# Another fixed order for the experts' ranks of load in a routed mixture of experts

## The chip, the core and the metric

The kernel runs on one core of one Trainium2 chip. It is measured in microseconds of device time for one execution; of several runs the median counts. Slower or faster always means this time.

## What is computed

One call computes two transformer blocks over 256 tokens of width 1024 in fp32. The first block mixes a short convolution, a gated delta rule and a stick-breaking attention, and has a dense feed-forward part; the second has two attentions and then a mixture of 32 experts. Only the mixture bears on this change:

```python
logits = hf @ w_router + b_router              # 256 tokens, 32 experts
top_val, top_idx = lax.top_k(logits, 4)        # each token goes to 4 experts
gates = softmax(top_val)
for each expert e, for the tokens x that chose it:
    hh = x @ w1[e] + b1[e]                     # 1024 -> 2048
    y  = swiglu_clamped(hh) @ w2[e] + b2[e]    # 1024 -> 1024
out[token] = sum of gate * y over its 4 experts
```

The weights of one expert (w1 of 8 MB and w2 of 4 MB) are read once, whatever the number of its tokens. The sum over the experts can be taken in any order.

## The kernel before

The dense parts come first and take a little over a third of the time. After the router the kernel counts the tokens of each expert and ranks the experts by that count; ranks 0 and 1 are fixed to experts 0 and 1, the others go from the largest load to the smallest. Each rank has a fixed number of slots, its capacity, from the table `CAPS`: ranks 0 and 1 have 64, ranks 2 and 3 have 128, ranks 4 to 7 have 96, ranks 8 to 17 have 64, ranks 18 to 31 have 32. Which expert stands at a rank is known only at run time; the program for each rank is written out in full. A loop at the end (line 1940) treats experts with more tokens than slots.

`ORDER` lists the ranks in the sequence in which the loop at line 1826 takes them; `pos` below is the place in that list. For each rank the loop emits:

- `selects` for the next rank (VectorE makes the one-hot matrices that pick its tokens and its gates),
- `first_rounds` of this rank: the product with w1, in blocks. `cut` cuts a capacity into blocks of 64 and 32 slots: 64 is one block, 96 is a block of 64 and one of 32, 128 is two blocks of 64. A block of 64 has two rounds, the first of slabs 0 and 1, the second of slabs 2 and 3; a block of 32 has one round, of all four. The matmuls stand at line 1725. Before the last round of a rank the next rank's tokens are gathered (line 1683),
- `turn` for the next rank: its tokens are transposed and normalised (lines 1694 to 1703),
- `combine` of the rank before: its output goes into the sum over experts (line 1791),
- `second` of this rank: the product with w2, for blocks of 64 at line 1768, of 32 at line 1763.

The weights come in slabs of 2 MB, six for each rank: four of w1, two of w2. Ten slab buffers stand in SBUF. All slabs are loaded by one queue of DMA issues on SyncE (SP), in the order in which they will be used, by `load_m` (the DMA stands at line 246). A slab buffer is given back by `free_m`, which `first_rounds` and `second` call behind the matmuls that read the slab last, so only in the rank's last block; it then emits the load of the slab that comes ten places later into the same buffer:

```python
def free_m(keys):
    for k in keys:
        del m_slab[k]
        m_freed.add(m_num.pop(k))
    while state["freed"] in m_freed:
        load_m(state["next"], m_pool[state["freed"]])
        state["next"] += 1
        state["freed"] += 1
```

The load waits on SP until TensorE has done those matmuls, and the loads behind it in the queue wait too. Numbered over the whole mixture, the slabs are 0 to 191, and slab n + 10 takes the place of slab n.

Of the kernel before, what the change touches and what calls it, by code (L numbers as in the profile page):

```python
# [48 lines left out]

FIRST = 2  # L50
CAPS = [64] * 2 + [128] * 2 + [96] * 4 + [64] * 10 + [32] * 14
ORDER = [0, 1, 8, 18, 9, 2, 26, 10, 3, 27, 11, 4, 28, 12, 5, 19, 13, 6, 29, 14, 7, 20, 15, 30, 21, 16, 22, 17, 23, 24, 25,
         31]


N_DENSE = 67
# [110 lines left out]
def kernel(ctx: ExitStack, tc: tile.TileContext, x_in, cols_in, rows_in, const_in, cona_in, conb_in, rpb_in,  # L167
# [62 lines left out]
    def load_m(m, pool=None):  # L230

        pos, i = divmod(m, 6)
        if pos >= len(ORDER):
            return
        rank = ORDER[pos]
        i = ((0, 2, 1, 3) if CAPS[rank] == 32 else (0, 1, 2, 3))[i] if i < 4 else i
# [1556 lines left out]
    def by_rank(rank):  # L1793
        if rank < FIRST:
            return lambda c: place[:, c, rank:rank + 1], lambda c: gate[:, c, rank:rank + 1]
        return lambda c: rp[:, 0, c, rank:rank + 1], lambda c: rp[:, 1, c, rank:rank + 1]

    def selects(pos):
        rank = ORDER[pos]
        pos_, gate_ = by_rank(rank)  # L1800
        return [select(w, first, tb, pos_, gate_ if pos else None) for first, tb in cut(CAPS[rank])]
# [23 lines left out]
    pend = []  # L1825
    for pos, rank in enumerate(ORDER):
        m0_ = 6 * pos
# [7 lines left out]
        n = 0  # L1835
        last = pos + 1 == len(ORDER)

# [263 lines left out]
```

## Time and profile before

| | us |
|---|---|
| median of 3 runs | 1496.65 (1492.77 to 1497.12) |
| the profiled execution | 1493.93 |
| its span, first to last instruction | 1492.1 |
| TensorE (PE) busy in the span | 1370.7 (92%) |
| VectorE (DVE) busy | 546.6 (37%) |
| ScalarE (ACT) busy | 455.9 (31%) |
| 192 slabs of experts' weights, 2048 KB each | 384 MB |
| first matmul with experts' weights | starts at 547.7 |

Times in the views count from the start of the span. TensorE's busy share is taken from modelled ends of its instructions, so the share is read with care. The mixture lies between 548 us and the end; the first ten slabs are on their way before it starts.

### The profile page before, as it was taken

The numbers are of one execution on the slowest core, as the hardware profiler recorded it, in microseconds if no ns is written. First come the engines' busy times: TensorE is split into PE (matmuls) and PEld (weight loads), VectorE is DVE, ScalarE is ACT, GpSimd is POOL, SyncE is SP. The second block draws the span as 40 slices with busy tenths as digits, with TensorE's granted clock in tenths as the row PEclk, the third lists the DMA queues.
The fourth block names the chain that finished last, engine by engine and source line by source line (L and its number), as shares of the span: only waits on it lengthen the run. The fifth ranks groups of instructions, "written<-read, shape, count | busy, mean of one in ns | idle before, by whom it ended". The sixth has DMA issues, their size and how long they took to land.

```text
span 1492.1 us, 21744 instructions
## 1 busy us (share of the span) xinstructions
PE 1370.7 (92%) x8859; PEld 736.1 (49%) x8863; DVE 546.6 (37%) x1258; ACT 455.9 (31%) x979; POOL 55.6 (4%) x31
## 2 busy tenths in 40 slices
PE   7999999999899999999999999999999987887674
PEld 6899789998678753333333333333333322222121
DVE  4755678776757841222122122112112111111112
ACT  5564465555556641111111111112111111101111
POOL 2322010000000000000000000000000000000000
PEclk9999999999999999999999999999999998989887
DMA  8322586656774599999899899999999999999994
GB/s 314 113 92 107 186 330 248 258 200 228 260 277 174 179 390 402 424 427 421 345 429 417 346 427 417 426 426 427 428 427 428 427 427 427 428 427 427 428 427 186
DMA packets 43433, 506.66 MB, mean 340 GB/s; under 512 B 5024, under 2 KB 5280, under 8 KB 6880
## 3 DMA queue, kind: packets, MB, share of 16 engines
q1 hardware_dynamic: 42464, 503.49, 82.5%
q10 hardware_dynamic: 864, 1.72, 0.4%
q8 instruction: 72, 1.18, 0.3%
q14 instruction: 33, 0.27, 0.0%
HBM read 504.14 MB, written 1.05 MB: 339 GB/s over the span
## 4 chain that ended last, share of the span: by engine, by line
PE 74%; DMA 17%; ACT 4%; DVE 3%; issue 1%; POOL 0%; SPq 0%; ACTq 0%; DVEq 0%; POOLq 0%
PE mm L1725 23%; DMA w<-in_we 16%; PE mm L447 15%; PE mm L1768 9%; PE acc L1791 4%; PE mm L1683 3%; PE mm L1763 3%; PE acc L481 3%; PE acc L482 3%; PE acc L483 3%; DMA w<-in_ws 1%; PE mm L824 1%; ACT aT L1746 1%; PE mm L1694 1%; PE mm L1730 1%
## 5 line engine op out<-in xcount | busy, mean ns | idle before, releaser
L1725 PE MATMUL mm<-w,xT 128*64 128x512 f32 (+1 forms) x2432 | 449.4, 642 | 56.3 <-DMA w<-in_we 56.0
L1725 PEld LDWEIGHTS mm<-w,xT 128*64 128x64 f32 (+1 forms) x2432 | 134.1, 131 | 354.2 <-issue 279.6
L1734 DVE TENSOR_SCALAR h<-mm 128x256 f32<-128x256 f32 x58 | 24.6, 425 | 714.8 <-PE mm L1730 714.8
L447 PE MATMUL mm<-hT,u 128*128 128x256 f32 x2064 | 263.5, 287 | 1.4 <-DVE hT L436 0.6
L447 PEld LDWEIGHTS mm<-hT,u 128*128 128x128 f32 x2064 | 254.1, 193 | 12.8 <-issue 8.4
L1735 ACT ACTIVATE a<-h 128x256 f32<-128x256 f32 x58 | 24.2, 417 | 506.0 <-DVE h L1734 506.0
L408 DVE TENSOR_TENSOR u<-w,u 128x1024 fp32r<-128x1024 f32 x115 | 145.5, 1270 | 67.3 <-ACT u L403 67.3
L403 ACT ACTIVATE u<-w 128x1024 fp32r<-128x1024 f32 x134 | 139.9, 1056 | 34.0 <-PE acc L483 23.9
L1768 PE MATMUL mm<-w,aT 128*64 128x512 f32 x640 | 143.2, 600 | 5.3 <-ACT aT L1746 5.3
L1768 PEld LDWEIGHTS mm<-w,aT 128*64 128x64 f32 x640 | 44.5, 138 | 91.2 <-issue 81.0
L1773 ACT ACTIVATE y<-mm 128x512 f32<-128x512 f32 x38 | 22.7, 597 | 208.6 <-PE mm L1768 139.8
L1763 PE MATMUL mm<-w,aT 128*32 128x512 f32 x576 | 65.5, 595 | 9.9 <-ACT aT L1746 9.9
L1683 PE MATMUL mm<-x,S 128*32 128x256 f32 (+1 forms) x448 | 57.4, 463 | 2.5 <-DVE S L1670 2.5
L408 POOL TENSOR_TENSOR u<-w,u 128x1024 fp32r<-128x1024 f32 x19 | 46.8, 2465 | 330.5 <-PE mm L306 201.4
L1063 DVE SCALAR_TENSOR_TENSOR fcv<-mm,cols,fcv 128x255 f32<-128x255 f32 x88 | 42.3, 481 | 22.9 <-ACT fcv L1060 21.4
L1701 ACT ACTIVATE xT<-mm,mod,gs 128x64 f32<-128x64 f32 (+1 forms) x152 | 46.6, 386 | 2.1 <-PE mm L1694 1.5
L1703 DVE TENSOR_SCALAR xT<-mm,gs,mod 128x64 f32<-128x64 f32 (+1 forms) x152 | 38.7, 321 | 3.0 <-PE mm L1694 3.0
L1763 PEld LDWEIGHTS mm<-w,aT 128*32 128x32 f32 x576 | 16.8, 109 | 46.5 <-issue 31.1
L1683 PEld LDWEIGHTS mm<-x,S 128*32 128x32 f32 (+1 forms) x448 | 18.7, 119 | 39.6 <-issue 33.1
L1926 POOL TENSOR_TENSOR fs<-fs,x 128x512 f32<-128x512 f32 x1 | 1.3, 1259 | 946.9 <-ACT fr L314 946.9
L1060 ACT ACTIVATE fcv<-mm,cols 128x256 f32<-128x256 f32 x44 | 20.7, 471 | 50.8 <-PE mm L447 50.8
L481 PE MATMUL acc<-u,gh 128*128 128x512 f32 x88 | 34.9, 397 | 0.0
(546 smaller groups left out, 1374.5 us busy)
## 6 DMA issues: line engine op xcount, KB each, us to landing
w<-in_we SPq DMA_DIRECT2D x192, 2048.0 KB, 23.3
w<-in_ws SPq DMA_DIRECT2D x90, 1024.0 KB, 5.3
nb<-in_rpb SPq DMA_DIRECT2D x4, 512.0 KB, 7.7
x<-in_x SPq DMA_DIRECT2D x2, 512.0 KB, 6.1
w<-in_ws SPq DMA_DIRECT2D x2, 512.0 KB, 7.5
bt<-in_b SPq DMA_DIRECT2D x3, 256.0 KB, 8.5
out<-fs SPq DMA_DIRECT2D x3, 256.0 KB, 2.1
grow<-in_wf ACTq DMA_DIRECT2D x1, 512.0 KB, 4.9
```

What stands on the lines that cost most here:

```text
L403: nc.scalar.activation(hi, raw, AF.Copy)
L408: eng.tensor_tensor(lo, raw, hi, op=OP.subtract)
L447: nc.tensor.matmul(b[:, 0:T], w[:, k, :], h[:, k, :], start=(n == 0), stop=(n == 3 * KC - 1))
L481: nc.tensor.matmul(o, th[:, kc, t], wh[:, w], start=first, stop=False)
L482: nc.tensor.matmul(o, th[:, kc, t], wl[:, w], start=False, stop=False)
L483: nc.tensor.matmul(o, tl[:, kc, t], wh[:, w], start=False, stop=last)
L1683: nc.tensor.matmul(b[p * tb:(p + 1) * tb, 0:n], S[:, c, p * tb:(p + 1) * tb], x[:, c, p * n:(p + 1) * n], start=(c == 0), stop=(c == 1))
L1701: nc.scalar.activation(dst, src, AF.Identity, scale=gs[:, kc:kc + 1], bias=mod[:, 24 + kc:25 + kc])
L1725: nc.tensor.matmul(b[p * tb:(p + 1) * tb, :], xT[:, k, q * tb:(q + 1) * tb], w1(p * nr + rd, kc // 4)[:, kc % 4, :], start=(kc == 0), stop ...
L1763: nc.tensor.matmul(b[p * tb:(p + 1) * tb, :], aT[:, 0, j, p0 * tb:(p0 + 1) * tb], w2(bi)[:, j, h * 512:(h + 1) * 512], start=(bi == 0), st ...
L1768: nc.tensor.matmul(b[p * tb:(p + 1) * tb, :], aT[:, rd, j, p0 * tb:(p0 + 1) * tb], w2(bi)[:, j, p * 512:(p + 1) * 512], start=(bi == 0 and ...
L1791: nc.tensor.matmul(acc[c][h], lhsT, rhs, start=False, stop=False, skip_group_check=True)
```

## The change

The list `ORDER` is replaced by another permutation of the same 32 ranks. Nothing else is changed: the capacities, the slabs, the buffers, the instructions of each rank and the code that stands at fixed places of the loop (after `pos` 0, 2, 3 and 6) stay. Ranks 0 and 1 remain first and rank 31 remains last.

```diff
 FIRST = 2
 CAPS = [64] * 2 + [128] * 2 + [96] * 4 + [64] * 10 + [32] * 14
-ORDER = [0, 1, 8, 18, 9, 2, 26, 10, 3, 27, 11, 4, 28, 12, 5, 19, 13, 6, 29, 14, 7, 20, 15, 30, 21, 16, 22, 17, 23, 24, 25,
-         31]
+ORDER = [0, 1, 18, 19, 8, 9, 10, 20, 2, 21, 22, 23, 4, 24, 11, 12, 5, 25, 6, 26, 13, 27, 7, 14, 15, 28, 3, 29, 30,
+         16, 17, 31]
```

Written as capacities, by `pos` from 0 to 31:

```
before: 64 64 64 32 64 128 32 64 128 32 64 96 32 64 96 32 64 96 32 64 96 32 64 32 32 64 32 64 32 32 32 32
after:  64 64 32 32 64 64 64 32 128 32 32 32 96 32 64 64 96 32 96 32 64 32 96 64 64 32 128 32 32 64 64 32
```

## Rows read from the trace of the kernel before

**Rows 1.** The page: rate of DMA in 40 slices; the slabs' issues, KB, us to landing.

```profile
GB/s 314 113 92 107 186 330 248 258 200 228 260 277 174 179 390 402 424 427 421 345 429 417 346 427 417 426 426 427 428 427 428 427 427 427 428 427 427 428 427 186
w<-in_we SPq DMA_DIRECT2D x192, 2048.0 KB, 23.3
```

**Rows 2.** Chain that ended last, from 1200 us: start, us, what.

```profile
1207.69 7.09 PE mm L1768 x32
...
1215.75 39.07 DMA w<-in_we
```

**Rows 3.** Windows: busy us of PE, PEld, DVE, ACT, POOL; PE clock, DMA, GB/s.

```profile
695.00:745.00 50.00, 49.36 (x284) 17.11 (x282) 9.23 (x28) 7.85 (x22) 0.00 (x0) 1.00 0.88 365
745.00:795.00 50.00, 48.17 (x248) 16.80 (x246) 10.33 (x35) 7.69 (x20) 0.00 (x0) 1.00 1.01 428
795.00:840.00 45.00, 44.36 (x258) 15.24 (x256) 7.90 (x23) 6.74 (x19) 0.00 (x0) 1.00 0.86 351
...
885.00:910.00 25.00, 24.74 (x166) 8.44 (x162) 6.46 (x20) 3.64 (x11) 0.00 (x0) 1.00 0.99 409
910.00:1215.00 305.00, 295.49 (x1844) 100.57 (x1846) 62.23 (x202) 51.84 (x143) 0.00 (x0) 1.00 1.01 427
1215.00:1462.00 247.00, 185.63 (x1081) 57.05 (x1073) 31.83 (x102) 28.71 (x79) 0.00 (x0) 0.87 1.01 427
```

**Rows 4.** Waits of the SP queue, 704 to 731 us: total, times, longest us.

```profile
SPq L246 <- PE mm L1768: 14.7, 1, 14.7
```

**Rows 5.** Issue and landing (us later) of slabs 17, 35, 43 and 44.

```profile
L246 SPq DMA_DIRECT2D w<-in_we x1: 333/333/333, 587.8 to 587.8; - x1
DMA to landing us min/median/max: 10.1/10.1/10.1
...
L246 SPq DMA_DIRECT2D w<-in_we x1: 333/333/333, 661.9 to 661.9; - x1
DMA to landing us min/median/max: 24.7/24.7/24.7
...
L246 SPq DMA_DIRECT2D w<-in_we x1: 331/331/331, 714.7 to 714.7; - x1
DMA to landing us min/median/max: 11.6/11.6/11.6
...
L246 SPq DMA_DIRECT2D w<-in_we x1: 333/333/333, 730.0 to 730.0; - x1
DMA to landing us min/median/max: 9.0/9.0/9.0
```

**Rows 6.** PE in order of time, first round of experts: start, us.

```profile
580.67 7.09 PE L1725 MATMUL mm<-w,xT 128*64 128x512 f32 x32
...
607.26 7.04 PE L1725 MATMUL mm<-w,xT 128*64 128x512 f32 x32
...
637.82 8.02 PE L1725 MATMUL mm<-w,xT 128*32 128x512 f32 x64
...
654.80 7.09 PE L1725 MATMUL mm<-w,xT 128*64 128x512 f32 x32
...
685.21 7.04 PE L1725 MATMUL mm<-w,xT 128*64 128x512 f32 x32
...
735.02 7.07 PE L1725 MATMUL mm<-w,xT 128*32 128x512 f32 x64
...
751.23 7.09 PE L1725 MATMUL mm<-w,xT 128*64 128x512 f32 x32
...
877.45 7.04 PE L1725 MATMUL mm<-w,xT 128*64 128x512 f32 x32
...
892.60 7.05 PE L1725 MATMUL mm<-w,xT 128*32 128x512 f32 x64
...
916.72 7.07 PE L1725 MATMUL mm<-w,xT 128*32 128x512 f32 x64
```

**Rows 7.** PE in order of time from 1240 us: a capacity-64 expert behind a wait.

```profile
1270.25 8.78 PE L1725 MATMUL mm<-w,xT 128*64 128x512 f32 x32 [2.93 <-DMA w<-in_we]
```

## The prediction

> **What bounds the kernel now.** I read the page first, then the chain that ended last, the windows of the mixture, the SP queue's waits, single slab issues, and TensorE in order of time. The page shows a DMA rate of about 427 GB/s through most of the mixture, with dips to 345 and 346 [rows 1]. The chain shows two regimes. Up to 1215 us it runs over TensorE; from 1215.75 us on it runs over the slab loads [rows 2]. So the end is set by when the last slab lands, and the last slab lands when the queue has moved 384 MB: any time in which the queue had nothing to move is in the total. In the windows the full rate is 428 GB/s [rows 3]. Below that lie, before the DMA-bound tail:
>
> - 695 to 745 us: 365 GB/s, so 50 x (1 - 365/428) = 7.4 us lost
> - 795 to 840 us: 351 GB/s, so 45 x (1 - 351/428) = 8.1 us lost
> - 885 to 910 us: 409 GB/s, so 25 x (1 - 409/428) = 1.1 us lost
>
> Together 16.6 us. From 910 to 1215 us the rate is 427, at most 0.7 us lost; the tail is at 427 too. The page's slice from 559.5 to 596.9 us has 402 GB/s [rows 1], another 37.3 x (1 - 402/428) = 2.3 us, at `pos` 0 and 1, which both orders share.
>
> The reader is to see in the SP queue why: the queue's longest wait in 704 to 731 us is 14.7 us, for the second product's matmul [rows 4]. That is `pos` 5, a rank of 128 slots. It gives its slabs back only in its second block, and its w2 slabs only at its end. Ten buffers are full by then.
>
> **A rule for a stall, from the rows.** A slab takes 2048 x 1024 bytes / 428 GB/s = 4.9 us, an expert six of them, 29.4 us. A slab issued into an empty queue landed 9.0 us after its issue [rows 5]. Let x be the time from a rank's first matmul to the landing of its sixth slab (negative: landed before). The 128 at `pos` 5 starts at 685.2 [rows 6]; its sixth slab, number 35, landed at 661.9 + 24.7 = 686.6 [rows 5], so x = 1.4. Its first w2 buffer came free at 730.0, 44.8 us after the start, and the load into it, slab 44, landed at 44.8 + 9.0 = 53.8. At an unbroken rate it was due nine slabs behind the sixth: x + 44.1 = 45.5. So 8.3 us are lost; the rows show slab 43 at 714.7 + 11.6 = 726.3 and slab 44 at 739.0 [rows 5], 12.7 us apart where 4.9 are due: 7.8 lost. The rule fits. From it:
>
> - 128 slots: no stall if x is at least 53.8 - 44.1 = 9.7.
> - 96 slots: its first slabs come free half way through its second block, at 892.6 + 3.5 - 877.45 = 18.7 us [rows 6], and land at 27.7; due at x + 24.5. No stall from x = 3.2 up.
> - 64 and 32 slots: a slab is free 3.6 us after the start, lands at 12.6, due at x + 24.5. No stall from x = -11.9 up.
>
> **What a rank does to x.** x grows by 29.4 less the rank's period, first matmul to first matmul. Periods in which TensorE waited for no load [rows 6]: 64 slots 607.26 - 580.67 = 26.6; 32 slots 751.23 - 735.02 = 16.2, and 17.0 at `pos` 3; 128 slots 735.02 - 685.21 = 49.8; 96 slots 916.72 - 877.45 = 39.3. A rank in front of a two-block rank takes 3.8 us more, for the larger gather and turn (64 before 128: 685.21 - 654.80 = 30.4); I take the same behind 32. A first matmul can't run before its first slab, so x is at most 5 x 4.9 = 24.5; past that TensorE waits and the loads run at full rate.
>
> **The change, part by part.** The list alone changes. Each rank issues the same instructions and the same six loads, in the one SP queue, so nothing is removed or added: bytes, matmuls and the tail behind rank 31 are the same, and those cost nothing more. What moves is where x stands at each rank. The loop's fixed work behind `pos` 2 now follows a rank of 32; before, the next rank's period was preceded by one of 30.6 (637.82 - 607.26) where a 64 takes 26.6 [rows 6], so I charge 17 + 4 = 21 us at most, 18 as the value nearest to the rows of a 32, to `pos` 2.
>
> The new ledger. `pos` 2 starts as before: slab 17 landed at 587.8 + 10.1 = 597.9 [rows 5], the start is 607.3, x = -9.4, above -11.9: no stall. Then:
>
> - `pos` 3 (32): -9.4 + 29.4 - 18 = 2.0 (at the upper bound of 21: -1.0). `pos` 4: 2.0 + 29.4 - 17 = 14.4. `pos` 5, 6, 7 behind 64s: 17.2, 20.0, 22.8.
> - `pos` 8, the first 128, behind a 32: 22.8 + 29.4 - 20.0 is over the cap, so x = 24.5. It needs 9.7. In it TensorE waits for its own slabs: slab four lands at 14.7 and is wanted at 10.6, so its w2 comes free 4.1 us later, 48.9, lands at 57.9, due at 68.6. Spare: 10.7 us.
> - `pos` 9: 24.5 + 29.4 - 53.9 = 0, needs -11.9. Two 32s bring it to the cap again. `pos` 12 (96): 24.5, needs 3.2. `pos` 13: 10.5, `pos` 14: 23.7, `pos` 16 (96): about 23, `pos` 18 (96) behind one 32: about 20, `pos` 22 (96): 24.5.
> - `pos` 23: 10.5; 64, 64: 13.3, 16.1; the 32 before the second 128 adds 29.4 - 20.0: cap. `pos` 26 (128): 24.5, spare 10.7 as before. Two 32s behind it, then 64, 64, 32 with x at the cap: the end waits for the loads.
>
> No rank stalls the queue behind `pos` 2. So the 16.6 us go, and the last slab lands that much earlier. What is late next is the queue itself at 428 GB/s, and TensorE waits for it from `pos` 7 on where before it did from 1215 us: that waiting costs nothing while x is positive. The sum: 1493.93 - 16.6 = 1477.3 us for the profiled execution. The median of the runs stands 2.7 above it, which gives 1480.0. I say 1478.5, between the two.
>
> Bounds of the sum: small dips in the windows (0.7 us in 910 to 1215) may stay or go, and the stalls by the rule add to 8.3 + 8.3 + 1.1 = 17.7 rather than 16.6. With the runs' spread of about 4 us this gives 1474 to 1482.
>
> **The rivals.**
>
> *A. The clock takes the cover away (slower).* TensorE now waits for loads from `pos` 7 on, so a rank can start at a low clock. In the tail before, the granted clock is 0.87 against 1.00 while TensorE was fed [rows 3], and the first round of a 64 behind a wait took 8.78 us [rows 7] instead of 7.09 [rows 6], 1.7 us more where a whole round at half rate would be 7 more. If a 128 starts so, its w2 is 1.7 to 3.4 us later, well inside the spare of 10.7. It decides from 10.7 us more per 128, and the change loses once both exceed it by 8.3 us, that is 19 us more each. Were the clock at 1.2 GHz through a whole 128, w2 would be free near 94 and land at 103 instead of 68.6: 34 us lost, twice, less 16.6: 1545 us. The rows speak against it, since two blocks on end are dense work. The Trainium skill, "TensorE: Matmul & The Clock Gate", section "HAM oscillation — how this bites in real kernels", says that a tile whose compute is shorter than the wait for its data has the clock fall in each wait, so that every tile starts at half rate. By that rule each rank of 32 starts cold; the trace agrees in the tail (0.87), and shows that a dense round wins the clock back. Chance 0.04.
>
> *B. Part of the stall returns.* If the 32 before a 128 or a 96 takes far more than 20 us, or the 128 itself some 15 more (gather, turn and select of two blocks behind waits that no row shows), each 128 could lose 3 to 5 us again: 6 to 10 us gained, 1484 to 1490 us. Against it: the cap holds x at 24.5 with up to 8 us to spare. Chance 0.08.
>
> *C. No change.* The lost rate would have to be the memory's own and not the full buffers'. The SP queue's wait of 14.7 us on a matmul [rows 4] speaks against it. About 1496. Chance 0.05.
>
> *D. More is gained:* the tail's last rounds at a better clock (1 to 2 us) and the early 2.3 us too: 1473. Chance 0.03.
>
> **How the numbers follow.** My forecast, no stall behind `pos` 2, has 0.80. A difference under 0.3%, 4.5 us, can't be told from no change. Forecast, B and D are faster: 0.91, of which I take 0.02 off for B's upper end: 0.89. C and that end: 0.07. A: 0.04. The range goes from D's 1473 to the middle of B, 1487.
>
> **What the profile of the changed kernel would show.** The windows between 690 and 910 us at 426 to 428 GB/s; the SP queue's waits for line 1768 short or hidden behind loads still under way; waits of line 1725 for slabs beginning near 720 to 750 us instead of 1215; the chain over the loads from there; a granted clock below 1.00 from there; the last slab landing near 1455 us and some 20 us of tail as before. I am wrong if the rate dips at `pos` 8 or 26 (first matmuls near 750 and 1280 us), or if a rank of 128 takes over 64 us.

## The result and the profile after

The changed kernel takes 1478.95 us (median of 4 runs, 1477.45 to 1480.36) against 1495.02 us for the kernel before in the same comparison: 16.1 us less, a ratio of 0.9894 with a 95% interval of 0.988 to 0.9908. Its profiled execution took 1480.36 us, with a span of 1478.5. VectorE and ScalarE are busy as long as before (546.4 and 456.3 us), TensorE 13.4 us less (1357.3); what changed is when the slabs arrive.

The page of the changed kernel: the rate of DMA in 40 slices, and the slabs' issues.

```profile
GB/s 317 114 89 99 200 330 231 270 213 229 239 262 221 171 349 388 429 426 427 427 429 426 428 426 427 429 426 429 426 429 425 429 426 427 428 427 428 427 427 156
w<-in_we SPq DMA_DIRECT2D x192, 2048.0 KB, 35.8
```

The two dips to 345 and 346 [rows 1] are gone: from the 17th slice to the one before last the rate lies between 425 and 429. A load now takes a median of 35.8 us from issue to landing where it took 23.3. That is no slower transfer, since landings still follow one another by 4.9 us; the loads are issued earlier and queue behind one another.

Windows of the changed kernel, over the same stretches as [rows 3] and to the end of the loads: length, busy us of PE, PEld, DVE, ACT, POOL, granted clock, DMA share, GB/s.

```profile
600.00:690.00 90.00, 86.58 (x536) 30.63 (x532) 19.78 (x70) 15.03 (x41) 0.00 (x0) 1.00 1.01 428
690.00:745.00 55.00, 46.95 (x247) 14.76 (x243) 7.61 (x25) 6.36 (x17) 0.00 (x0) 0.94 1.01 427
745.00:795.00 50.00, 45.34 (x242) 15.54 (x243) 11.80 (x38) 7.75 (x23) 0.00 (x0) 1.00 1.01 427
795.00:840.00 45.00, 42.93 (x322) 14.71 (x318) 8.34 (x30) 8.01 (x22) 0.00 (x0) 1.00 1.01 427
840.00:1215.00 375.00, 335.08 (x2056) 110.31 (x2056) 68.28 (x222) 57.64 (x158) 0.00 (x0) 0.98 1.01 427
1215.00:1450.00 235.00, 213.16 (x1192) 72.87 (x1192) 42.43 (x132) 35.13 (x95) 0.00 (x0) 0.98 1.00 426
```

The stretches that ran at 365, 351 and 409 GB/s [rows 3] run at 427. TensorE's idle time has moved: before, it was busy without waits for loads up to 1215 us; now 8 of the 55 us from 690 to 745 are idle, and the granted clock is 0.94 there. The chain that ended last, from 600 us, shows the same from the other side (start, us, what):

```profile
617.95 3.64 PE mm L1763 x32
621.59 0.06 PE mm L1628
621.65 28.03 DMA w<-in_we
649.77 0.03 issue
649.80 39.18 DMA w<-in_we
```

The chain changes from TensorE to the loads at 621.65 us; before it did at 1215.75 [rows 2].

The first 128, now at `pos` 8, is the place where a stall would show. TensorE of the changed kernel in order of time, its rounds (L1725) and its second product (L1768):

```profile
753.01 3.65 PE L1725 MATMUL mm<-w,xT 128*64 128x512 f32 x16
757.42 3.65 PE L1725 MATMUL mm<-w,xT 128*64 128x512 f32 x16 [0.75 <-DMA w<-in_we]
762.40 3.65 PE L1725 MATMUL mm<-w,xT 128*64 128x512 f32 x16 [1.11 <-DMA w<-in_we]
767.21 3.65 PE L1725 MATMUL mm<-w,xT 128*64 128x512 f32 x16 [1.15 <-DMA w<-in_we]
...
797.81 7.09 PE L1768 MATMUL mm<-w,aT 128*64 128x512 f32 x32 [0.39 <-ACT aT L1746]
805.71 7.05 PE L1725 MATMUL mm<-w,xT 128*32 128x512 f32 x64
```

Issue and landing (us later) of its sixth slab (53), and of the first slab loaded into one of its w2 buffers (62):

```profile
L246 SPq DMA_DIRECT2D w<-in_we x1: 332/332/332, 737.9 to 737.9; - x1
DMA to landing us min/median/max: 39.0/39.0/39.0
...
L246 SPq DMA_DIRECT2D w<-in_we x1: 333/333/333, 801.5 to 801.5; - x1
DMA to landing us min/median/max: 20.1/20.1/20.1
```

The reader is to see three things. TensorE waits for its own slabs in the first two rounds, four halves in steps of about 4.9 us. The sixth slab landed at 737.9 + 39.0 = 776.9, so x is 23.9. And the load into the first free w2 buffer was issued 801.5 - 753.0 = 48.5 us after the start; it took 20.1 us to land because other loads were still under way ahead of it. In the 128 before, the same load found an empty queue and landed 9.0 us after its issue [rows 5]. The SP queue's wait for the second product, from 786 to 802 us, is as long as the one in [rows 4]:

```profile
SPq L246 <- PE mm L1768: 14.7, 1, 14.7
```

So it is not that wait that has gone. Slab 61 landed at 816.7, 15 us after the wait was over at 801.5, where before slab 43 had landed at 726.3, 3.7 us before it was over at 730.0 [rows 5].

### The profile page after: what moved, and what is told of

Same layout as the page of the kernel before. It is cut to its first block, busy times and chain, and to the rows that moved or that the text cites. A ratio compares the mean times of both kernels' runs of the same rounds, so it can differ in the third digit from the quotient of the medians.

```text
span 1478.5 us, 21750 instructions
## 1 busy us (share of the span) xinstructions
PE 1357.3 (92%) x8859; PEld 731.9 (49%) x8863; DVE 546.4 (37%) x1258; ACT 456.3 (31%) x979; POOL 55.6 (4%) x31
## 4 chain that ended last, share of the span: by engine, by line
PE 53%; DMA 40%; DVE 3%; ACT 3%; issue 1%; SPq 0%; POOL 0%; ACTq 0%; DVEq 0%; POOLq 0%
DMA w<-in_we 39%; PE mm L447 15%; PE mm L1725 11%; PE mm L1768 5%; PE acc L481 3%; PE acc L482 3%; PE acc L483 3%; PE acc L1791 2%; PE mm L1763 1%; PE mm L1683 1%; PE mm L824 1%; DMA w<-in_ws 1%; DVE u L408 1%; PE mm L497 1%; PE mm L306 0%
## 5 line engine op out<-in xcount | busy, mean ns | idle before, releaser
L1725 PE MATMUL mm<-w,xT 128*64 128x512 f32 (+1 forms) x2432 | 435.6, 615 | 55.6 <-DMA w<-in_we 54.8
L1725 PEld LDWEIGHTS mm<-w,xT 128*64 128x64 f32 (+1 forms) x2432 | 130.4, 127 | 343.8 <-issue 257.7
L403 ACT ACTIVATE u<-w 128x1024 fp32r<-128x1024 f32 x134 | 139.9, 1056 | 34.5 <-PE acc L483 23.9
L1768 PE MATMUL mm<-w,aT 128*64 128x512 f32 x640 | 143.2, 600 | 5.7 <-ACT aT L1746 5.7
L1768 PEld LDWEIGHTS mm<-w,aT 128*64 128x64 f32 x640 | 44.5, 138 | 91.6 <-issue 81.1
L1063 DVE SCALAR_TENSOR_TENSOR fcv<-mm,cols,fcv 128x255 f32<-128x255 f32 x88 | 42.3, 481 | 23.0 <-ACT fcv L1060 21.4
## 6 DMA issues: line engine op xcount, KB each, us to landing
w<-in_we SPq DMA_DIRECT2D x192, 2048.0 KB, 35.8
```

What stands on the lines that cost most here:

```text
L403: nc.scalar.activation(hi, raw, AF.Copy)
L1063: nc.vector.scalar_tensor_tensor(t[:, sh:], b[:, :T - sh], w(2 - sh), t[:, sh:], op0=OP.mult, op1=OP.add)
L1725: nc.tensor.matmul(b[p * tb:(p + 1) * tb, :], xT[:, k, q * tb:(q + 1) * tb], w1(p * nr + rd, kc // 4)[:, kc % 4, :], start=(kc == 0), stop ...
L1768: nc.tensor.matmul(b[p * tb:(p + 1) * tb, :], aT[:, rd, j, p0 * tb:(p0 + 1) * tb], w2(bi)[:, j, p * 512:(p + 1) * 512], start=(bi == 0 and ...
```

## The experiments

Kernels e1 to e4 hold the list in one line, so their line numbers behind it are one lower (L1724 for L1725).

**e1: two swaps in the old order.**

```diff
-ORDER = [0, 1, 8, 18, 9, 2, 26, 10, 3, 27, ..., 15, 30, 21, 16, 22, 17, 23, 24, 25, 31]
+ORDER = [0, 1, 8, 18, 9, 30, 26, 10, 22, 27, ..., 15, 2, 21, 16, 3, 17, 23, 24, 25, 31]
```

> The order of before with two swaps alone: rank 2 (128 slots, pos 5) changes places with rank 30 (pos 23), rank 3 (128, pos 8) with rank 22 (pos 26). Theory (a 128 stalls the loads when its sixth slab lands less than 9.7 us after its first matmul): with two ranks of 32 in the 128s' old places x is over 20 at both new places and at every 96, so all of the gain is there: 1476 to 1481 us, 0.988 to 0.991 of before, no gap between landings over 2 us behind pos 2. Rival (the gain comes from taking small ranks first at pos 2 and 3 and from the whole rearrangement): at most half of the gain, 1487 or more.

Measured: 1480.32 us, ratio 0.9902 (0.9883 to 0.9921). Two swaps give what the whole new list gives, within the intervals. Windows of e1:

```profile
690.00:745.00 55.00, 44.27 (x268) 14.73 (x266) 11.54 (x40) 9.16 (x27) 0.00 (x0) 0.94 1.01 427
745.00:795.00 50.00, 36.16 (x204) 9.75 (x204) 3.81 (x14) 4.57 (x12) 0.00 (x0) 0.86 1.01 427
795.00:840.00 45.00, 37.35 (x212) 12.81 (x214) 11.09 (x38) 8.23 (x24) 0.00 (x0) 0.96 1.01 429
```

By issue, landing and first matmul, x was 22.0 at the first moved 128 (sixth slab landed at 1222.0, first matmul at 1199.9) and 11.9 at the second (1310.1 and 1298.2). That second value was expected to be over 20 and was not, since a 64 and a 32 stand between the two; it was still over 9.7, and the queue did not stall. So a 128 need not find x at its cap.

**e2 and e3: the first 128 at `pos` 3 and at `pos` 4.**

```diff
-ORDER = [0, 1, 18, 19, 8, 9, 10, 20, 2, ...]
+ORDER = [0, 1, 18, 2, 8, 9, 10, 20, 19, ...]    # e2: 128 behind one 32
+ORDER = [0, 1, 18, 19, 2, 9, 10, 20, 8, ...]    # e3: 128 behind two 32s
```

> The changed kernel with ranks 2 (128) and 19 (32) swapped, so that a 128 stands at pos 3 behind one 32. Theory: x at pos 3 is 0 to 4, under 9.7, so the queue stalls for 6 to 12 us in this rank and the two behind it: 1486 to 1491 us. Rival (any place behind a small rank will do): 1479.

> The changed kernel with ranks 2 (128) and 8 (64) swapped, so that a 128 stands at pos 4 behind two 32s. Theory: x at pos 4 is 11 to 15, just over 9.7, and the ranks behind it stay above -11.9, so there is no stall: 1478 to 1480 us as the changed kernel. Rival (a 128 needs TensorE to have caught up with the loads altogether, or three and more small ranks ahead): 5 us or more lost, 1484 or more.

Measured: e2 1489.5 us, ratio 0.9975 (0.9957 to 0.9993); e3 1477.95 us, ratio 0.9889 (0.9869 to 0.9909). With the 128 one place later the kernel is 11.6 us faster. A window of e2 over the 128:

```profile
640.00:690.00 50.00, 49.36 (x244) 18.01 (x242) 9.12 (x27) 6.90 (x18) 0.00 (x0) 1.00 0.85 348
```

First round of e2's 128, and issue and landing of its sixth slab (23):

```profile
628.35 7.09 PE L1724 MATMUL mm<-w,xT 128*64 128x512 f32 x32
L245 SPq DMA_DIRECT2D w<-in_we x1: 332/332/332, 615.9 to 615.9; - x1
DMA to landing us min/median/max: 13.1/13.1/13.1
```

Windows of e3:

```profile
600.00:690.00 90.00, 85.58 (x530) 30.29 (x528) 20.07 (x72) 15.07 (x41) 0.00 (x0) 1.00 1.01 427
690.00:745.00 55.00, 54.37 (x272) 19.31 (x270) 10.36 (x32) 7.96 (x22) 0.00 (x0) 1.00 1.01 428
```

In e2 x at the 128 was 0.6, so the rule gives 9.7 - 0.6 = 9.1 us; the window lost 50 x (1 - 348/428) = 9.3. The SP queue's wait for the second product, 14.9 us, is no sign of this by itself, since the changed kernel has it too. In e3 x was 12.7 (landed at 656.3, first matmul at 643.56) and nothing was lost.

**e4: the large ranks last.**

```diff
+ORDER = [0, 1, 18, 19, ..., 29, 30, 8, 9, ..., 16, 17, 4, 5, 6, 7, 2, 3, 31]
```

> The changed kernel with all small ranks first and the large ones at the end: 0, 1, 18 to 30, 8 to 17, 4, 5, 6, 7, 2, 3, 31. Theory: x is at its cap until the four 96s, each of which takes 10 to 14 from it; at the third and fourth 96 and both 128s it is far below the thresholds, the queue stalls for 50 us or more, and the end waits for TensorE: 1530 to 1550 us. Rival (small ranks first is what helps): no slower than the changed kernel, 1479.

Measured: 1577.66 us (2 runs), ratio 1.0555 (1.0523 to 1.0588). "Small ranks first" alone is thus 83 us worse than the old order. The direction is the theory's, the size was underrated, by some 28 us even against the upper end. Windows of e4:

```profile
600.00:1340.00 740.00, 611.40 (x3484) 196.79 (x3482) 123.74 (x414) 99.47 (x276) 0.00 (x0) 0.92 1.01 427
1340.00:1450.00 110.00, 104.76 (x624) 35.53 (x622) 20.25 (x66) 16.98 (x44) 0.00 (x0) 1.00 0.71 289
1450.00:1520.00 70.00, 68.04 (x337) 23.91 (x334) 12.54 (x37) 9.62 (x25) 0.00 (x0) 1.00 0.61 240
1520.00:1576.00 56.00, 40.88 (x233) 13.93 (x231) 11.85 (x31) 11.99 (x31) 1.26 (x1) 0.93 0.06 21
```

The rate holds at 427 GB/s up to 1340 us, falls to 289 and 240 while the six large ranks follow one another, and the loads are done near 1520, with 56 us of work behind them. Two windows lose 36 and 31 us. Issue and landing of the last slab:

```profile
L245 SPq DMA_DIRECT2D w<-in_we x1: 333/333/333, 1511.3 to 1511.3; - x1
DMA to landing us min/median/max: 9.2/9.2/9.2
```

It landed at 1520.5, 62.0 us later than in the changed kernel, so the stalls alone lie within what was expected (1530 to 1550 is 51 to 71 us above 1479). What the expectation left out is the work behind it: 57.9 us to the end of the span (1578.4) instead of 20.0. A 96 in front of a 96 took 45.3 us (first matmuls at 1256.23 and 1301.50), 3.2 of them waits for its own slabs; 39.4 to 43.4 had been expected.

**e5 and e6: more work on TensorE in each 128.**

```diff
         combine_pend()
+        if CAPS[rank] == 128:
+            keep_warm(36)        # e6: 94; idle matmuls of about 0.21 us
         for b_, a in zip(blks, acts):
```

> The changed kernel with 36 idle matmuls (bf16, 128x512, about 0.21 us each, 7.7 us) in front of the second product of each of the two 128s; they write a bank that nobody reads. Theory: the spare at a 128 is 10.7 us, so its w2 buffers still come free in time: no stall, 1478 to 1481 us. Rival (TensorE's time in the large ranks counts): 2 x 7.7 = 15 us more, 1494.

> The same with 94 idle matmuls, 20 us. Theory: 20 - 10.7 = 9.3 us of stall at each 128, 1497 us (1493 to 1501), with the two gaps at the first load into a w2 buffer of the 128s, slabs 62 and 170. Rival (TensorE's time counts in full): 40 us more, 1519. Rival (nothing there counts): 1479.

Measured: e5 1479.34 us, ratio 0.9899 (0.9879 to 0.9919); e6 1495.59 us, ratio 1.0012 (1.0 to 1.0025). Twice 7.7 us more (8.05 in the trace) cost nothing that can be measured; twice 20 us (20.7) cost 16.6. Windows of e6 behind its two 128s:

```profile
800.00:830.00 30.00, 29.36 (x175) 11.02 (x176) 0.00 (x0) 2.79 (x7) 0.00 (x0) 1.00 0.71 290
...
1340.00:1375.00 35.00, 34.36 (x210) 13.08 (x209) 1.10 (x3) 3.47 (x10) 0.00 (x0) 1.00 0.73 300
```

Issue and landing of slab 62 in e6:

```profile
L246 SPq DMA_DIRECT2D w<-in_we x1: 333/333/333, 820.8 to 820.8; - x1
DMA to landing us min/median/max: 7.9/7.9/7.9
```

The first of these windows in e5:

```profile
800.00:830.00 30.00, 29.08 (x232) 10.23 (x234) 3.50 (x12) 5.26 (x14) 0.00 (x0) 1.00 1.01 427
```

In e5 the first loads into a w2 buffer of the two 128s, slabs 62 and 170, landed 4.9 us behind the loads before them, as in an unbroken queue. 30 x (1 - 290/428) = 9.7 and 35 x (1 - 300/428) = 10.5 us are lost in e6, at the w2 buffers of the two 128s, where 9.3 each were expected. The spare at a 128 is real and about as large as worked out.

**e7: the clock kept up.**

```diff
+                if R == 4 and kc == 3:
+                    keep_warm(14)
                 if free and kc % 4 == 3:
```

> The changed kernel with 14 idle matmuls (3 us) between the two halves of each round of a block of 32, where TensorE waits for slabs. Theory: the granted clock rises towards 1.00 in the DMA-bound stretch, the first rounds shorten, and the time stays within 0.2%, 1476 to 1482 us, since the loads set the end. Rival (the low clock costs time): 3 us or more faster than the changed kernel.

Measured: 1478.36 us, ratio 0.9891 (0.9871 to 0.9911). Windows of e7, to be set beside the last two of the changed kernel:

```profile
840.00:1215.00 375.00, 354.81 (x2198) 120.44 (x2188) 68.50 (x223) 58.24 (x159) 0.00 (x0) 1.00 1.01 427
1215.00:1450.00 235.00, 226.29 (x1280) 77.61 (x1278) 42.41 (x132) 35.15 (x95) 0.00 (x0) 1.00 1.00 425
```

The clock went from 0.98 to 1.00 and the time stayed: what TensorE does while it waits for slabs is free either way.

**e8: the old order, both blocks of a rank together in the second product.** The loop over the four pieces of w2 stands outside, the loop over the blocks inside, each block with its own bank.

```diff
-        for b_, a in zip(blks, acts):
-            pend.append((b_, second(w, b_, a, w2, free if b_ is blks[-1] else None)))
+        pend += second_all(w, blks, acts, w2, free)
...
+        for bi, bl in enumerate(BO):
+            for (R, tb, xT, gT_), aT, b in zip(blks, aTs, bs):
...
+            if bi % 2:
+                free([4 + bi // 2])
```

> The kernel before, in its order, with the two blocks of a rank taken together in the second product (each slab of w2 is read by both blocks and then given back). Theory: the first w2 buffer of a 128 comes free about 41 us behind its first matmul instead of 44.8, so each of its two stalls falls from 8 to about 4.5 us: 1484 to 1489 us. Rival (the late release of the w1 slabs, or the place of the ranks itself, is what costs): as before, 1494.

Measured: 1491.35 us (median of 10 runs; one of them took 6724.62 us, is not in the ratio and has no trace), ratio 0.9978 (0.9963 to 0.9992): better than before, and less than expected. Windows of e8 over the stretches of [rows 3]:

```profile
695.00:745.00 50.00, 49.47 (x298) 17.39 (x298) 11.68 (x38) 8.23 (x23) 0.00 (x0) 1.00 0.96 393
745.00:795.00 50.00, 48.70 (x238) 17.05 (x232) 9.46 (x28) 7.73 (x20) 0.00 (x0) 1.00 0.99 419
795.00:840.00 45.00, 44.47 (x272) 15.69 (x272) 10.08 (x34) 7.82 (x22) 0.00 (x0) 1.00 0.93 374
```

Issue and landing of slabs 44 and 45 in e8:

```profile
L246 SPq DMA_DIRECT2D w<-in_we x1: 333/333/333, 721.1 to 721.1; - x1
DMA to landing us min/median/max: 7.9/7.9/7.9
...
L246 SPq DMA_DIRECT2D w<-in_we x1: 333/333/333, 728.0 to 728.0; - x1
DMA to landing us min/median/max: 8.8/8.8/8.8
```

The first w2 buffer of the 128 came free at 721.1 instead of 730.0, and the loss in the first window fell from 7.4 to 4.1 us. But the second buffer now follows 6.9 us behind the first, so slab 45 came 7.8 us after slab 44 where 4.9 are due: a second, smaller gap. It was missing from my expectation, which had looked at the first buffer alone. The late release of w2 is a cause of the stalls, shown; earlier release of one buffer alone doesn't take them away.

**e9 and e10: the remaining early gap, and the changed kernel again beside it.** The product of the gates with the second bias moves from `pos` 0 to `pos` 7, its operand gets a tile of its own, and the first combine starts the sums.

```diff
-        if pos == 0:
+        if pos == 7:
             for c in range(2):
                 for h in range(2):
-                    nc.tensor.matmul(acc[c][h], gateT[:, c * P:(c + 1) * P], b2[h], start=True, stop=False,
+                    nc.tensor.matmul(acc[c][h], gateT[h * NE:(h + 1) * NE, c * P:(c + 1) * P], b2[h], start=False, stop=False,
...
-        nc.tensor.matmul(acc[c][h], lhsT, rhs, start=False, stop=False, skip_group_check=True)
+        nc.tensor.matmul(acc[c][h], lhsT, rhs, start=(c, h) not in begun, stop=False, skip_group_check=True)
+        begun.add((c, h))
```

> The changed kernel with the eight matmuls of the experts' second bias (line 1880, 3.6 us on TensorE) moved from pos 0 to pos 7, where TensorE waits for loads; the first combine starts the sums instead. Theory: the rank at pos 1 starts 3.6 us earlier, its x rises from -13 to about -9.5, above the threshold of -11.9, and the gaps of 1 to 2 us at slabs 14 to 17 go: 2 to 3.5 us less than the changed kernel beside it. Rival (those gaps are the loads' own start): no change against it.

> The changed kernel as it is, on the same chip as the one beside it, for the difference between the two: 1477 to 1481 us.

Measured: e9 1477.24 us, ratio to before 0.989 (0.9871 to 0.9909); e10 1480.18 us, 0.9907 (0.989 to 0.9925). e9 is 2.9 us below e10; of six runs each, the slowest of e9 (1479.81) is the only one above the fastest of e10 (1478.96). No interval was taken between the two, and their intervals to before overlap. The traces show where the queue lost less. One window of e9:

```profile
560.00:600.00 40.00, 38.90 (x206) 14.59 (x204) 8.98 (x29) 6.91 (x21) 0.00 (x0) 1.00 1.01 424
```

The same window of e10:

```profile
560.00:600.00 40.00, 39.14 (x188) 14.59 (x184) 8.51 (x28) 6.57 (x21) 0.00 (x0) 0.96 0.97 398
```

The same window of e5, which starts as the changed kernel does:

```profile
560.00:600.00 40.00, 38.91 (x196) 14.62 (x192) 8.97 (x29) 6.91 (x21) 0.00 (x0) 1.00 1.00 419
```

40 x (1 - 398/428) = 2.8 us were lost in e10 and 0.4 in e9; x at `pos` 1 was -13.9 in e10 and -7.7 in e9, above the threshold of -11.9. But the granted clock differs too, 0.96 in e10 and 1.00 in e9. With the bias in its old place and the clock at 1.00 there, e5 lost 0.8 us, and e3 and e7 (405 and 414 GB/s) 2.1 and 1.3. So e9 lost least, and part of what it gained on e10 may be the clock's; no run separates the two. e9 has the lowest median of this study, 0.7 us below e3, with overlapping runs.

## Why the prediction was right

The forecast was 1478.5 us, and 1478.95 was measured. Step by step:

- *The end is set by the last slab, and the stalls of the queue are in the total.* Right: the three slow stretches are at full rate, the last slab was issued at 1419.5 and landed 39.0 us later, at 1458.5 (foretold: near 1455), and 20.0 us of tail follow, where before it landed at 1471.7 with 20.4 behind it.
- *The rule for a stall at a 128, x of at least 9.7.* Held in e1 to e3: 0.6 lost 9.3 us where the rule gives 9.1 (e2), 11.9 and 12.7 lost nothing (e1, e3). The second 128 of the kernel before, from which the rule was not taken, had x = 1.5, and two landings there came 2.3 and 5.9 us late: 8.2 where the rule gives 8.2. Between 1.5 and 11.9 none stands, so the threshold itself is bracketed and not measured. Of its terms, the 9.0 us from issue to landing in an empty queue is the softest: 7.5 to 7.9 in e4 and e6. The rule for a 96 was met in e4: the third one had x = -7.8, for which it gives 3.2 + 7.8 = 11.0 us, and the load into its first freed buffer (slab 172) landed 16.1 us behind the one before, 11.2 lost.
- *The ledger of x.* By the same working as at `pos` 8, the trace after has 3.8 and 18.1 at `pos` 3 and 4 (foretold 2.0 and 14.4), 23.9 and 24.3 at the two 128s (24.5 each), and 24.3, 22.8, 21.4 and 23.2 at the four 96s (24.5, about 23, about 20, 24.5). The early values were too low, partly since slab 17 landed 1.8 us later, so that x at `pos` 2 was -7.5 and not -9.4, partly because I took 17.0 us for a 32; the one at `pos` 3 took 641.42 - 625.39 = 16.0 between first matmuls. The 18 us for `pos` 2 came out (18.1), but no row had given it: it was a choice between 17 and 21, and lucky.
- *Spare of 10.7 us at a 128.* w2 came free 48.5 us after the start, foretold 48.9. e5 and e6 confirm the spare from both sides.
- *The size, 16.6 us.* The medians differ by 16.1, the two profiled executions by 1493.93 - 1480.36 = 13.6. The 3.0 us that are missing there are in the queue's own times. It started worse (393 GB/s from 559.5 to 597 us, 3.1 us lost, against 2.3 [rows 1]), so that slab 17 landed at 599.7 instead of 597.9 [rows 5]. From there to the last slab it took 858.8 us where it took 873.8: 15.0 less and not 16.6, because small slips cost more than before (last section). The tail gave 0.4. So the sum of 1477.3 for the profiled execution was 3.1 too low, and that 1478.5, put between two values, came within 0.5 of the median is partly luck: the four runs spread over 2.9 us.
- *Rival A, the clock.* Not borne out: the granted clock did fall, to 0.94 in one window, but e7 took that away and the time stayed. The Trainium skill, "TensorE: Matmul & The Clock Gate", section "HAM oscillation — how this bites in real kernels", has the clock fall in waits for data; the trace agrees that it falls, and e7 that the fall costs nothing where the loads are the bound. The case needed 19 us more per 128; the period of the first was 805.71 - 753.01 = 52.7 us against 49.8, and the 2.9 us are waits for its own slabs. From 560 to 600 us, where TensorE sets the pace, e7 shows nothing; the clock was 0.96 there and 3.1 us were lost; the executions with 1.00 in that stretch lost 0.4 to 2.1 (e9).
- *Rivals B and C* have nothing left to stand on: no gap returned, and the lost rate was not the memory's own. The reason given against C was weak, though: the wait of 14.7 us stands in the changed kernel as well. *Rival D* needed the early stall to go as well; in e9, where it nearly did, the median was 1477.24, not 1473.
- *Signs foretold.* TensorE was to wait for loads from 720 to 750 us on; it did so from about 728, after two short waits of 0.42 and 1.15 us at 698 and 708. The SP queue's waits for line 1768 were to be short or hidden; they were as long as before, and hidden. The chain was to run over the loads from there; it did so from 621.65 already. The prediction had SP wait for TensorE alone, but in this trace no load of the mixture was issued before the one eight places ahead of it had landed (slab 43 at 689.1, slab 35 landed at 689.0), so the chain of a load that is waited for runs back over earlier loads. Issue to landing is at most 40.1 us behind `pos` 2, about eight times 4.9.

## What to carry to other kernels

Where one queue streams weights through a ring of buffers that are given back in order, keep a ledger: at each step, the time at which its last buffer lands less the time at which its work starts. Steps that hold buffers for longer than their loads take must meet a high value, and steps that hold them for less restore it; order them so that the ledger stays between the stall threshold and the cap. What counts is the next threshold, not small first or large first: two swaps did all of it, and taking that maxim to its end cost 83 us.

## What was not expected of the hardware

Even where the queue always had loads waiting, single landings came 0.4 to 1.2 us later than 4.9 us behind the one before, nine times in the changed kernel behind `pos` 3, about 7 us in all. Before, such slips cost about 4 us apart from the stalls. All nine follow within 7 us on a 16 KB packet of the instruction queue (q8 on the page, 72 packets in the whole execution), which took about 1.0 us on its DMA engine where a weight packet of the same size takes 0.61. But 36 such packets lie in that stretch, and most were followed by no slip. That these fetches delay the slab is an inference from the times; no run here separates it.
